# Mixer of a two-layer hybrid diffusion step: S5 gates ahead of the glu products, products out of the state in four bands, result read back on SyncE's queue, convolution branch last

## The chip, the cores and the metric

The kernel runs on one core of one Trainium2 chip. The metric is device time in microseconds (us), the median of several runs of the whole program, lower is better. The engines are PE (TensorE, matrix products), DVE (VectorE), ACT (ScalarE), POOL (GpSimd) and SP (SyncE), which here only issues transfers; ACT and POOL have queues for transfers too.

## What is computed

Two layers over 384 tokens (128 context, 256 latent), width 1024. A layer is half a SwiGLU feed-forward block, a mixer and another half block, each behind a modulated norm. The change lies in the mixer:

```python
def _mixer(h, P, l, h0):
    z = h @ P['w_in'][l]
    z_a, z_b, z_c = jnp.split(z, [S5_WIDTH, S5_WIDTH + 2 * CONV_WIDTH], axis=-1)
    y_a, h_final = _s5_branch(z_a, P, l, h0)      # 512 wide
    y_b = _conv_branch(z_b, P, l)                 # 256 wide, 31 taps, layer norm, silu
    y_c = _sgmlp_branch(z_c, P, l)                # 256 wide
    gates = jax.nn.sigmoid(h @ P['w_gate'][l] + P['b_gate'][l])
    g_a, g_b, g_c = jnp.split(gates, N_BRANCH, axis=-1)
    merged = (g_a * (y_a @ P['w_br_a'][l]) + g_b * (y_b @ P['w_br_b'][l])
              + g_c * (y_c @ P['w_br_c'][l]))
    return merged @ P['w_out'][l], h_final
```

The S5 branch is a complex diagonal state-space scan in both directions over 32 groups of 16 channels with 64 states, then `y = gelu(C s + d*z)` and `y * sigmoid(y @ w_glu)`.

## The kernel before

Every large product is made of three float32r products, high times high, high times low, low times high (L198, L199, L200), over 384 token columns. Weights come in units of 128 x 1024 numbers: SP's queue loads `wr` (512 KB), ACT rounds it to `wh` (L126), DVE subtracts to get `wl` (L105). Each of the three has three buffers, and units are fetched two ahead. A unit is 24 matmuls on PE, or 12 where the contraction is 256 deep (the branches b and c). Within a unit all four k of output block m = 0 come first, then those of m = 1. An activation operand is likewise a pair: `hh`/`hl` (normed input, and later the merged sum), `ah`/`al` (the S5 branch), `yc` and `yb` pairs.

PE's order is the program's. The order on the other engines is a fixed list that the framework's scheduler makes from the program, so a statement that moves in the program can move its rows on DVE and ACT past others.

A mixer's units, numbered from 1: w_in 1 to 12; then for n = 0 to 3 a gate c unit pair and a branch c unit (13 to 24); gate b 25 to 32; then the list `LAST`; then w_out 51 to 58. In `LAST`, "gate" is a pair of units of the S5 gate, "glu" one unit of the S5 output product, "a" and "b" the branch products of S5 and convolution. Before, LAST puts gate 0, 1 in units 33 to 36, glu 0, 1 in 37, 38, gate 2 in 39, 40, a 0, a 1 in 41, 42, gate 3 in 43, 44, a 2 in 45, b 0, b 1 in 46, 47, a 3 in 48, b 2, b 3 in 49, 50. An "a" result is multiplied by its sigmoid gate and added into `acc`, then a "b" result; when a block has both, `hh`/`hl` of it are split off, and w_out needs them in order of k.

Beside the units run the steps of `side()`: after each unit one entry of its `plan` is executed. The S5 scan goes through it in four quarters q of 8 groups: `load_to` (weights `ms`), `to_state` (products L1172 into a bank, then copies into `m_xs`), `rotate` and `scan` on DVE (`m_t`, two scans L1215, L1216, then `m_hh`), `load_from` (weights `my`, `mi`), `from_state` (products L1249, copy `m_ysb` on ACT, transfers to `y_d` in DRAM on ACT's queue and back to `m_yt` on POOL's), `activate` (transposes L138, then y, its gelu, `zp`, `ah`, `al`). The convolution's 31 taps (`cacc`), the longest chain of DVE rows, and its layer norm (`csq`, `csd`, `crs`, `cn`, ending in `yb`) are entries of the plan too. Small products given to `small` are popped one list after each triple of matmuls.

In `from_state` the 48 columns of U or `hh` are stationary and 128 weight columns move, once for each half of the bank:

```python
pe.matmul(b[64 * half : 64 * half + NCH, g * P : (g + 1) * P], u, w, ...)
```

## Time and profile before

| | |
|---|---|
| median of 3 runs | 1775.85 us (1775.21 to 1778.99) |
| profiled execution, its own time | 1775.03 us |
| its span, first to last instruction | 1773.0 us |
| mean granted clock of TensorE | 0.997 |
| PE busy | 1743.7 us, 98% |
| DVE busy | 1246.8 us, 70% |
| ACT busy | 795.8 us, 45% |
| POOL busy | 203.5 us, 11% |
| layer 0's mixer | some 345 to 616 us, with w_out |
| layer 1's mixer | some 1230 to 1490 us |

The profile is of one execution. A busy share is an average over the whole span; a stage can have another limit than the average shows, so the windows and the waits are read beside it. A matmul's listed duration overlaps the next one, so costs on PE are read from start to start.

### The profile page before, as it was taken

The page shows a single profiled execution, that of the slowest core. Times are in us where ns is not written, and L with a number is a line of the kernel's source. Part 1 is how long each engine was busy: PE and PEld are TensorE (multiplying, and loading weights), DVE is VectorE, ACT ScalarE, POOL GpSimd, SP SyncE. Part 2 cuts the span into 40 slices and gives each one's busy share as a digit, 9 for nine tenths or more (in the row PEclk, how much of TensorE's full clock was granted, in tenths as well). Part 3 has the DMA queues.
Part 4 walks back from the last instruction along what each step waited for, and adds up shares of the span by engine and source line. Part 5 has one row for each costly group of instructions (what it writes and reads, how often), then busy time and mean ns, then how long its engine had stood idle before and what let it go on. Part 6 is the DMA issues. An engine that isn't in the chain of part 4 may idle for free.

```text
span 1773.0 us, 30946 instructions
## 1 busy us (share of the span) xinstructions
PE 1743.7 (98%) x12116; PEld 1652.8 (93%) x12116; DVE 1246.8 (70%) x2344; ACT 795.8 (45%) x1330; POOL 203.5 (11%) x400
## 2 busy tenths in 40 slices
PE   7999999999999999999999999999999999999997
PEld 4899999999999989999999899999999999999997
DVE  5496676778986885678487666767799788544435
ACT  3344333575355553233366233336744546423233
POOL 2012343310010000000001133232100000000000
PEclk9999999999999999999999999999999999999999
DMA  9778788776753677788346776667666443444332
GB/s 343 249 224 275 231 252 269 226 198 190 240 157 108 186 238 228 237 280 257 112 131 208 234 224 215 175 195 233 162 210 200 131 123 116 132 130 127 123 125 77
DMA packets 253753, 344.48 MB, mean 194 GB/s; under 512 B 22399, under 2 KB 216651, under 8 KB 253608
## 3 DMA queue, kind: packets, MB, share of 16 engines
q1 hardware_dynamic: 228504, 299.18, 53.4%
q0 software_dynamic: 17088, 39.51, 7.5%
q10 hardware_dynamic: 8016, 3.82, 0.8%
q8 instruction: 95, 1.56, 0.4%
q14 instruction: 50, 0.41, 0.1%
HBM read 309.75 MB, written 32.70 MB: 193 GB/s over the span
## 4 chain that ended last, share of the span: by engine, by line
PE 81%; DVE 10%; ACT 4%; DMA 3%; issue 2%; SPq 0%; ACTq 0%; DVEq 0%
PE mm L198 25%; PE mm L200 25%; PE mm L199 25%; PE ax L386 3%; DVE wl L105 3%; DVE cacc L123 2%; DMA wr<-in_w_gate_dram 1%; DVE m_t L105 1%; PE tb L138 1%; ACT wh L126 1%; DVE m_hh L105 1%; DMA modw<-in_w_mod_dram 1%; DVE macc L123 1%; DMA wr<-in_w_in_dram 1%; ACT zp L1125 0%
## 5 line engine op out<-in xcount | busy, mean ns | idle before, releaser
L105 DVE TENSOR_TENSOR wl<-wr,wh 128x1024 fp32r<-128x1024 f32 (+2 forms) x389 | 457.0, 1175 | 352.1 <-ACT wh L126 347.4
L126 ACT ACTIVATE wh<-wr 128x1024 fp32r<-128x1024 f32 (+1 forms) x387 | 395.9, 1023 | 613.9 <-PE mm L199 443.9
L198 PE MATMUL mm<-hh,wh 128*128 128x384 f32 x1840 | 625.3, 340 | 2.7 <-ACT hh L621 2.7
L200 PE MATMUL mm<-hh,wl 128*128 128x384 f32 x1840 | 617.1, 335 | 4.4 <-DVE wl L105 4.2
L199 PE MATMUL mm<-hl,wh 128*128 128x384 f32 x1840 | 616.3, 335 | 0.5 <-DVE hl L105 0.3
L198 PEld LDWEIGHTS mm<-hh,wh 128*128 128x128 f32 x1840 | 345.9, 188 | 31.7 <-issue 18.1
L200 PEld LDWEIGHTS mm<-hh,wl 128*128 128x128 f32 x1840 | 345.8, 188 | 6.7 <-DVE wl L105 6.7
L199 PEld LDWEIGHTS mm<-hl,wh 128*128 128x128 f32 x1840 | 345.9, 188 | 1.2 <-DVE hl L105 1.1
L198 PE MATMUL mm<-ah,wh 128*128 128x384 f32 x800 | 273.2, 342 | 0.0
L199 PE MATMUL mm<-al,wh 128*128 128x384 f32 x800 | 269.4, 337 | 0.8 <-DVE al L105 0.8
L200 PE MATMUL mm<-ah,wl 128*128 128x384 f32 x800 | 270.0, 338 | 0.0
L198 PEld LDWEIGHTS mm<-ah,wh 128*128 128x128 f32 x800 | 150.2, 188 | 10.2 <-issue 6.7
L199 PEld LDWEIGHTS mm<-al,wh 128*128 128x128 f32 x800 | 150.4, 188 | 1.7 <-DVE al L105 1.1
L200 PEld LDWEIGHTS mm<-ah,wl 128*128 128x128 f32 x800 | 150.2, 188 | 0.0
L123 DVE SCALAR_TENSOR_TENSOR x<-mm,gt,x 128x128 f32<-128x128 f32 x224 | 83.1, 411 | 33.3 <-PE mm L200 33.1
L198 PE MATMUL mm<-xh,wh 128*128 128x386 f32 x240 | 84.7, 353 | 0.0
L126 ACT ACTIVATE ah<-av 128x384 fp32r<-128x384 f32 x82 | 42.1, 519 | 89.4 <-DVE av L105 89.1
L200 PE MATMUL mm<-xh,wl 128*128 128x386 f32 x240 | 81.9, 341 | 0.0
L199 PE MATMUL mm<-xl,wh 128*128 128x386 f32 x240 | 81.9, 341 | 0.0
L123 DVE SCALAR_TENSOR_TENSOR macc<-modw,silu_c,macc 128x1024 f32<-128x1024 f32 x56 | 69.9, 1278 | 14.9 <-DMA modw<-in_w_mod_dram 14.9
L123 DVE SCALAR_TENSOR_TENSOR cacc<-pad,pv,cacc 128x399 f32<-128x399 f32 x120 | 69.7, 627 | 0.0
L386 PE MATMUL ax<-modw,silu_c 128*32 128x512 f32 (+1 forms) x576 | 63.2, 511 | 0.7 <-DMA modw<-in_w_mod_dram 0.7
(316 smaller groups left out, 1820.0 us busy)
## 6 DMA issues: line engine op xcount, KB each, us to landing
wr<-in_ffn_w_dram SPq DMA_DIRECT2D x256, 512.0 KB, 3.6
modw<-in_w_mod_dram SPq DMA_DIRECT2D x144, 512.0 KB, 5.4
wr<-in_w_gate_dram SPq DMA_DIRECT2D x48, 512.0 KB, 3.8
wr<-in_w_in_dram SPq DMA_DIRECT2D x24, 512.0 KB, 3.6
my<-my POOLq DMA_DIRECT2D x16, 512.0 KB, 5.5
ms<-ms POOLq DMA_DIRECT2D x16, 512.0 KB, 4.9
m_ms<-ms SPq DMA_DIRECT2D x16, 512.0 KB
m_my<-my SPq DMA_DIRECT2D x16, 512.0 KB, 7.4
```

The costliest lines, as they stand in the source:

```text
L105: (eng or dve).tensor_tensor(out, a, b, op=op)
L123: dve.scalar_tensor_tensor(out, a, s, b, op0=op0, op1=op1)
L126: act.activation(hi, full, AF.Copy)
L138: pe.transpose(out, in_, ident[:rows, :rows])
L198: pe.matmul(out, wh[:, k, cols], xh, start=first, stop=False)
L199: pe.matmul(out, wh[:, k, cols], xl, start=False, stop=False)
L200: pe.matmul(out, wl[:, k, cols], xh, start=False, stop=last)
L386: pe.matmul(b[32 * s : 32 * s + 32, :w], silu_c[:, k, :], raws[i][:, c : c + w], start=(k == 0), stop=(k == KD - 1), skip_group_check=True,)
```

## The change

- `LAST` runs all four S5 gates first, then glu 0, 1, then a 0 to a 3, then b 0 to b 3. The S5 gates' sigmoids go to a tile of their own pool (`gate_a`).
- `to_state` gives both products to `small` as one list.
- `from_state` makes the weights stationary, 32 columns at a time, in four bands of the bank, and the 48 columns of U or `hh` move: 192 traced matmuls for each q instead of 48. The result already has channels on partitions; one copy and one transfer take it to `y_d`, whose layout is changed.
- `load_y`, a plan entry of its own, reads it back with eight transfers of 24 KB on SP's queue.
- `activate` has no transposes; y reads `m_yt` in SBUF, and the reordering of tokens moves into the write of `zp`.
- The plan is laid out anew: `load_to` ahead of `load_from`, `from_state` for q = 0 to 3 after units 17, 22, 27, 32 (before: 17, 21, 25, 29), `activate` after 22, 27, 32, 37 (before: 25, 27, 30, 33), the convolution's taps spread differently, its mean, variance and broadcast after 38, 41 and 43 (before: 36, 39, 41).

```diff
@@ -1077,8 +1077,8 @@
         return v.rearrange("p (j c) -> p j c", j=TC)
 
     LAST = [
-        ("gate", 0), ("gate", 1), ("glu", 0), ("glu", 1), ("gate", 2), ("a", 0), ("a", 1), ("gate", 3), ("a", 2),
-        ("b", 0), ("b", 1), ("a", 3), ("b", 2), ("b", 3),
+        ("gate", 0), ("gate", 1), ("gate", 2), ("gate", 3), ("glu", 0), ("glu", 1), ("a", 0), ("a", 1), ("a", 2),
+        ("a", 3), ("b", 0), ("b", 1), ("b", 2), ("b", 3),
     ]
 
     def mixer_srcs(l):
@@ -1112,7 +1112,7 @@
 
 
         zd = drm.tile([G, H, TC, NCH], F32, tag=f"z_d{l}", name="z_d")
-        yd = drm.tile([NT, G * H], F32, tag=f"y_d{l}", name="y_d")
+        yd = drm.tile([4, P, GB, NCH], F32, tag=f"y_d{l}", name="y_d")
         ld.start()
         hs = ld.hs
         zp = m6([P, 4, NT], "zp")
@@ -1185,9 +1185,11 @@
                 act.activation(XS[HI, i, :, 1:EC], bv[HI, :, CC - 1 :: -1], AF.Copy)
                 act.activation(XS[HI, i, :, EC + 1 :], bv[HI, :, NCH - 1 : CC - 1 : -1], AF.Copy)
 
+            place = []
             for i in range(2):
                 b = tb_bank()
-                small.append([partial(product, i, g, b) for g in range(GB)] + [partial(take, i, b)])
+                place += [partial(product, i, g, b) for g in range(GB)] + [partial(take, i, b)]
+            small.append(place)
 
         def rotate(q, part):
             d = st5[q]
@@ -1242,44 +1244,38 @@
 
             def product(g):
                 for n in range(3):
-                    for half in range(2):
-                        i = 4 * half + g
-                        u = U[:, q * GB + i, :] if n == 0 else hh[:, n - 1, i, :]
-                        w = mib[:, i, :] if n == 0 else d["my"][i // GS][:, i % GS, n - 1, :]
+                    u = U[:, q * GB + g, :] if n == 0 else hh[:, n - 1, g, :]
+                    w = mib[:, g, :] if n == 0 else d["my"][g // GS][:, g % GS, n - 1, :]
+                    for r in range(0, P, 32):
                         pe.matmul(
-                            b[64 * half : 64 * half + NCH, g * P : (g + 1) * P],
+                            b[r : r + 32, g * NCH : (g + 1) * NCH],
+                            w[:, r : r + 32],
                             u,
-                            w,
                             start=(n == 0),
                             stop=(n == 2),
                             skip_group_check=True,
                         )
 
             def take():
-                ysb = c2([P, TC, 4, H], "m_ysb")
-                bv = b.rearrange("p (g i h) -> p i g h", g=4, h=H)
-                yv = yd.rearrange("(c i) f -> c i f", i=TC)
-                for half in range(2):
-                    r = slice(64 * half, 64 * half + NCH)
-                    act.activation(ysb[r], bv[r], AF.Copy)
-                    f0 = q * P + 64 * half
-                    bq.dma_start(yv[:, :, f0 : f0 + 64], ysb[r].rearrange("c i g h -> c i (g h)"))
-                d["yt"] = c2([P, 3, P], "m_yt")
-                gq.dma_start(d["yt"], yd[:, q * P : (q + 1) * P].rearrange("(t p) f -> p t f", p=P))
-
-            small.append([partial(product, g) for g in range(4)] + [take])
+                ysb = c2([P, GB, NCH], "m_ysb")
+                act.activation(ysb, b[:, : GB * NCH].rearrange("p (g c) -> p g c", c=NCH), AF.Copy)
+                bq.dma_start(yd[q], ysb)
+
+            small.append([partial(product, g) for g in range(GB)] + [take])
+
+        def load_y(q):
+            d = st5[q]
+            d["yt"] = c2([P, TC, NCH], "m_yt")
+            for g in range(GB):
+                tq.dma_start(d["yt"][g * H : (g + 1) * H], yd[q, :, g, :].rearrange("(i h) c -> h i c", h=H))
 
         def activate(t):
-            b = tb_bank()
-            for n in range(3):
-                transpose(b[:, n * P : (n + 1) * P], st5[t]["yt"][:, n, :], P)
             y2 = tmp("y2")
-            ci = lambda v: v.rearrange("p (c i) -> p c i", i=TC)
-            stt(ci(y2), zp[:, t].rearrange("p (j c) -> p c j", j=TC), pv[:, 48 + t : 49 + t], ci(b[:, :NT]))
+            stt(y2, zp[:, t], pv[:, 48 + t : 49 + t], st5[t]["yt"].rearrange("p i c -> p (i c)"))
             ga = tmp("ga")
             gelu_sig(ga, y2)
             yg = zp[:, t]
-            mul(yg, y2, ga)
+            mul(yg.rearrange("p (c i) -> p i c", i=TC), jc(y2), jc(ga))
             ygs[t] = yg
             hl = a_pair()
             split(yg, *hl)
@@ -1477,31 +1473,33 @@
                 [f(sg_u, 0), f(sg_u, 1)],
                 [f(sg_gelu)],
                 [f(to_state, 0), f(sg_norm)],
-                [f(load_from, 0), f(rotate, 0, 0), f(rotate, 0, 1)],
-                [f(load_to, 1), f(scan, 0, 0), f(sg_mix), f(sg_out)],
+                [f(load_to, 1), f(rotate, 0, 0), f(rotate, 0, 1)],
+                [f(load_from, 0), f(scan, 0, 0), f(sg_mix), f(sg_out)],
                 [f(scan, 0, 1)],
-                [f(to_state, 1), tap[0]],
-                [f(load_to, 2), f(rotate, 1, 0), f(rotate, 1, 1)],
-                [f(from_state, 0), f(load_from, 1), f(scan, 1, 0)],
+                [tap[0]],
+                [f(to_state, 1)],
+                [f(load_to, 2), f(from_state, 0), f(rotate, 1, 0), f(rotate, 1, 1)],
+                [f(load_from, 1), f(scan, 1, 0)],
                 [f(scan, 1, 1)],
-                [f(to_state, 2), tap[1]],
-                [f(load_to, 3), f(rotate, 2, 0), f(rotate, 2, 1)],
-                [f(from_state, 1), f(load_from, 2), f(scan, 2, 0)],
+                [f(load_y, 0), tap[1]],
+                [f(to_state, 2), tap[2]],
+                [f(load_to, 3), f(from_state, 1), f(rotate, 2, 0), f(rotate, 2, 1)],
+                [f(load_from, 2), f(scan, 2, 0), f(activate, 0)],
                 [f(scan, 2, 1)],
-                [f(to_state, 3), tap[2]],
-                [f(rotate, 3, 0), f(rotate, 3, 1)],
-                [f(from_state, 2), f(load_from, 3), f(scan, 3, 0)],
-                [f(scan, 3, 1), f(activate, 0)],
-                [tap[3]],
-                [f(activate, 1)],
-                [f(from_state, 3), tap[4]],
-                [f(ctx_states), tap[5]],
-                [f(activate, 2)],
+                [f(load_y, 1), tap[3]],
+                [f(to_state, 3), tap[4]],
+                [f(from_state, 2), f(rotate, 3, 0), f(rotate, 3, 1)],
+                [f(load_from, 3), f(scan, 3, 0), f(activate, 1)],
+                [f(scan, 3, 1)],
+                [f(load_y, 2), tap[5]],
                 [tap[6]],
+                [f(from_state, 3)],
+                [f(ctx_states), f(activate, 2)],
                 [tap[7]],
-                [f(activate, 3), tap[8]],
+                [f(load_y, 3), tap[8]],
                 [tap[9]],
                 [tap[10]],
+                [f(activate, 3)],
                 [f(conv_mean)],
                 [f(conv_center)],
                 [],
@@ -1613,9 +1611,9 @@
         yfs = []
         for op, n in LAST:
             if op == "gate":
-                banks = gate(0, n)
-                for bank, bias in banks:
-                    gt = tmp("gt")
+                gat = c3([P, 2, NT], "gate_a")
+                for m, (bank, bias) in enumerate(gate(0, n)):
+                    gt = gat[:, m]
                     with tc.high_priority():
                         act.activation(gt, bank, AF.Sigmoid, bias=bias)
                     gts.append(gt)
```

The first place is DVE ahead of unit 25, the first unit of gate b 0, in layer 0. `cacc` are taps, `m_t` the rotation, L1217 and L1218 (L1215 and L1216 before) the two scans of one q, `wl` the low halves in order of units; the row of form 128x512 is unit 24. Before:

```order
L105 TENSOR_TENSOR acc<-mm,gt 128x384
L123 SCALAR_TENSOR_TENSOR cacc<-pad,pv_311,cacc 128x399 x4
L105 TENSOR_TENSOR wl<-wr,wh 128x512
L123 SCALAR_TENSOR_TENSOR cacc<-pad,pv_311,cacc 128x399 x3
L105 TENSOR_TENSOR wl<-wr,wh 128x1024
L123 SCALAR_TENSOR_TENSOR cacc<-pad,pv_311,cacc 128x399
L105 TENSOR_TENSOR m_t_5585<-m_rot,m_xs 128x400
```

After, between the same two `wl` (unit 24's is followed by three cacc, by y_5616 of `activate` and by one more cacc; these are the rows from there on):

```order
L105 TENSOR_TENSOR m_t_5455<-m_rot,m_xs 128x400
L105 TENSOR_TENSOR m_t_5456<-m_rot,m_xs 128x400
L105 TENSOR_TENSOR m_t_5457<-m_rot,m_xs 128x400
L105 TENSOR_TENSOR m_t_5455<-m_t_5455,m_t_5456 128x400
L105 TENSOR_TENSOR m_t_5458<-m_rot,m_xs 128x400
L1217 SCALAR_TENSOR_TENSOR m_t_5456<-m_rho,m_t_5455 128x400
L105 TENSOR_TENSOR m_t_5457<-m_t_5457,m_t_5458 128x400
L105 TENSOR_TENSOR m_t_5455<-m_rot,m_t_5456 128x400
L1218 SCALAR_TENSOR_TENSOR m_t_5458<-m_rho,m_t_5457 128x400
L123 SCALAR_TENSOR_TENSOR ga<-ga,y_5616 128x384
L105 TENSOR_TENSOR m_t_5457<-m_rot,m_t_5458 128x400
L105 TENSOR_TENSOR wl<-wr,wh 128x1024
```

Three taps stood between the two `wl` before; now four taps, y, ga and the whole rotation and scan of q = 2 stand there.

The second place is ACT around the glu products in layer 0. `cs` is the sigmoid of a glu product, `ah` the high half of the branch, `csd` the root of the convolution's variance. Before, from glu 0 on:

```order
L1626 ACTIVATE cs<-mm 128x384
L126 ACTIVATE ah<-zp 128x384
L1626 ACTIVATE cs<-mm 128x384
L126 ACTIVATE wh<-wr 128x1024
L126 ACTIVATE ah<-zp 128x384
L1626 ACTIVATE cs<-mm 128x384
L126 ACTIVATE ah<-zp 128x384
L126 ACTIVATE wh<-wr 128x1024
L1443 ACT_TABLE_LOAD
L1443 ACTIVATE csd<-ax,eps_t 128x3
L1620 ACT_TABLE_LOAD
L1620 ACTIVATE gt<-mm,pv_311 128x384
```

After:

```order
L126 ACTIVATE wh<-wr 128x1024
L1618 ACTIVATE gate_a<-mm,pv_311 128x384
L126 ACTIVATE wh<-wr 128x1024
L1439 ACT_TABLE_LOAD
L1439 ACTIVATE csd<-ax,eps_t 128x3
L1624 ACT_TABLE_LOAD
L1624 ACTIVATE cs<-mm 128x384 x2
L126 ACTIVATE wh<-wr 128x1024
L126 ACTIVATE ah<-zp 128x384 x2
L1624 ACTIVATE cs<-mm 128x384 x2
L126 ACTIVATE ah<-zp 128x384 x2
L126 ACTIVATE wh<-wr 128x1024
```

The root of the variance with its two table loads stood behind the four `cs`, with the gates; it now stands ahead of them.

The third place is DVE at the start of w_out, in layer 0. `gate_b` is the product of a "b" result with its gate, `hl` the low halves of the merged sum, in order of k (0, 1, 2, 3, ...). Before, from unit 50's `wl` on:

```order
L105 TENSOR_TENSOR wl<-wr,wh 128x512
L105 TENSOR_TENSOR gt<-mm,gt 128x384
L105 TENSOR_TENSOR hl_6618<-acc,hh_6617 128x384
L105 TENSOR_TENSOR hl_6624<-acc,hh_6623 128x384
L105 TENSOR_TENSOR acc<-acc,gate_b 128x384
L105 TENSOR_TENSOR gt<-mm,gt 128x384
L105 TENSOR_TENSOR acc<-acc,gate_b 128x384
L105 TENSOR_TENSOR gate_b<-mm,gate_b 128x384
L105 TENSOR_TENSOR hl_6650<-acc,hh_6649 128x384
L105 TENSOR_TENSOR hl_6656<-acc,hh_6655 128x384
L105 TENSOR_TENSOR gate_b<-mm,gate_b 128x384
L105 TENSOR_TENSOR wl<-wr,wh 128x1024
```

After, from the product of b 2 on (its first `wl` is unit 51's):

```order
L105 TENSOR_TENSOR gate_b<-mm,gate_b 128x384
L105 TENSOR_TENSOR hl_6942<-acc,hh_6941 128x384
L105 TENSOR_TENSOR hl_6948<-acc,hh_6947 128x384
L105 TENSOR_TENSOR gate_b<-mm,gate_b 128x384
L105 TENSOR_TENSOR wl<-wr,wh 128x1024
L105 TENSOR_TENSOR gate_b<-mm,gate_b 128x384 x2
L105 TENSOR_TENSOR acc<-acc,gate_b 128x384 x2
L105 TENSOR_TENSOR wl<-wr,wh 128x1024
L105 TENSOR_TENSOR hl_6974<-acc,hh_6973 128x384
L105 TENSOR_TENSOR hl_6980<-acc,hh_6979 128x384
```

The pair of `hl` for k = 2, 3 stood ahead of unit 51's `wl`; it now stands behind the last products of b 3, two sums and unit 52's `wl`.

## Rows read from the trace of the kernel before

**Rows 1.** The page: busy time, share of the span and instructions of each engine.

```profile
PE 1743.7 (98%) x12116; PEld 1652.8 (93%) x12116; DVE 1246.8 (70%) x2344; ACT 795.8 (45%) x1330; POOL 203.5 (11%) x400
```

**Rows 2.** Waits of PE: what it waited for, total us, times, longest us.

```profile
PE mm L200 <- DVE wl L105: 4.2, 5, 1.4
```

**Rows 3.** Windows: us, busy us (x instructions) of each engine, granted clock, DMA share, GB/s.

```profile
440.00:520.00 80.00, 77.75 (x774) 73.88 (x773) 79.79 (x145) 35.41 (x65) 9.17 (x15) 1.00 0.63 204
```

**Rows 4.** Timeline, PE, both product bursts: start us, us, engine, line, operation, tiles, form, count.

```profile
399.78 0.33 PE L200 MATMUL mm<-hh,wl 128*128 128x384 f32 x1
...
403.42 0.34 PE L200 MATMUL mm<-hh,wl 128*128 128x384 f32 x1
403.69 0.89 PE L1172 MATMUL tb<-U,m_ms 128*32 128x48 f32 x64
404.50 0.44 PE L198 MATMUL mm<-hh,wh 128*128 128x384 f32 x1
...
432.06 0.34 PE L200 MATMUL mm<-hh,wl 128*128 128x384 f32 x1
...
435.08 0.44 PE L198 MATMUL mm<-hh,wh 128*128 128x384 f32 x1
```

**Rows 5.** Timeline, DVE, one full stretch of layer 0's mixer.

```profile
477.15 0.97 DVE L1216 TENSOR_TENSOR_SCAN m_t<-m_rho,m_t 128x400 f32<-128x400 f32 x1
478.05 1.19 DVE L105 TENSOR_TENSOR wl<-wr,wh 128x1024 fp32r<-128x1024 f32 x1
479.17 0.56 DVE L105 TENSOR_TENSOR m_t<-m_rot,m_t 128x400 f32<-128x400 f32 x1
...
480.12 1.25 DVE L105 TENSOR_TENSOR m_hh<-m_t,m_t 64x128 f32<-64x128 f32 x4
...
485.36 0.91 DVE L123 SCALAR_TENSOR_TENSOR y<-zp,pv,tb 128x384 f32<-128x384 f32 x1
486.18 0.63 DVE L123 SCALAR_TENSOR_TENSOR cacc<-pad,pv,cacc 128x399 f32<-128x399 f32 x1
486.72 1.22 DVE L105 TENSOR_TENSOR wl<-wr,wh 128x1024 fp32r<-128x1024 f32 x1
```

**Rows 6.** Timeline, PE, the wait behind that stretch; [idle before <-releaser].

```profile
485.95 0.34 PE L200 MATMUL mm<-hh,wl 128*128 128x384 f32 x1
486.12 0.49 PE L138 MATMUL tb<-ident,m_yt 128*128 128x128 f32 x3
...
486.62 0.33 PE L199 MATMUL mm<-hl,wh 128*128 128x384 f32 x1
488.00 0.44 PE L200 MATMUL mm<-hh,wl 128*128 128x384 f32 x1 [1.04 <-DVE wl L105]
```

**Rows 7.** Timeline, end of the second glu product: PE, then ACT, then DVE.

```profile
539.17 0.34 PE L200 MATMUL mm<-ah,wl 128*128 128x384 f32 x1
...
539.37 1.06 ACT L126 ACTIVATE wh<-wr 128x1024 fp32r<-128x1024 f32 x1
540.34 0.51 ACT L126 ACTIVATE ah<-zp 128x384 fp32r<-128x384 f32 x1
...
544.62 1.28 ACT L1443 ACT_TABLE_LOAD   x1
...
543.22 0.56 DVE L105 TENSOR_TENSOR al<-zp,ah 128x384 fp32r<-128x384 f32 x1 [0.51 <-ACT ah L126]
```

**Rows 8.** Timeline, DVE, ahead of the output projection.

```profile
579.90 1.01 DVE L105 TENSOR_TENSOR hl<-acc,hh 128x384 fp32r<-128x384 f32 x2
...
581.30 1.22 DVE L105 TENSOR_TENSOR wl<-wr,wh 128x1024 fp32r<-128x1024 f32 x1
```

**Rows 9.** Windows and PE's timeline after the longest wait of layer 0's mixer.

```profile
360.61 0.37 PE L468 MATMUL ax<-ones,sqacc 128*32 128x1 f32 x24 [1.96 <-DVE sqacc L105]
...
360.50:362.00 1.50, 1.40 (x29) 1.38 (x30) 1.50 (x4) 1.21 (x2) 0.00 (x0) 0.81 1.10 397
362.00:364.50 2.50, 2.50 (x9) 2.50 (x8) 2.46 (x8) 0.00 (x0) 0.00 (x0) 0.50 0.74 226
```

## Prediction

> **What bounds the kernel now.** I read the page first: PE is busy 98% of the span [rows 1], so time moves only if PE gets less to do or waits more or less. PE's own waits come next. In the mixers the wait that recurs is for wl, the low half of a weight unit, which DVE makes [rows 2]: 4.2 us over the kernel, nearly all of it in two places, one per layer. The windows say why: from 440 to 520 us DVE is busy 79.79 of 80 us [rows 3]. In that stretch, "the wall" below, PE has next to no lead, and an instruction put in front of a wl is paid by PE. Outside it DVE has room, and what counts there is the length of a chain from one PE result to the next PE operand.
>
> The unit of account: a matmul of 384 columns takes 0.173 us start to start (399.78 to 403.42 us is 21 of them) [rows 4], so a weight unit of 24 takes PE 4.15 us and one of 12 takes 2.08.
>
> **Part 1, less work on PE (gain).** A burst of products pays for a change of shape at both ends: 403.42 to 403.69 is 0.27 instead of 0.173, and about the same again behind it, 0.2 in all; the 64 matmuls between take 0.81 us, 12.7 ns each [rows 4]. Merging the two lists of to_state drops one pair of changes for each of four q: 4 x 0.2 = 0.8. A from_state burst takes 435.08 - 432.06 - 0.17 = 2.85, 2.95 with the change behind it [rows 4]. Its replacement has 192 traced matmuls of exactly the form of the 64 priced above (32 stationary columns, 48 moving): 192 x 12.7 ns + 0.2 = 2.64, so 0.31 less, four times: 1.25. The three transposes of activate cost 486.62 - 485.95 less two matmuls, 0.33 [rows 6], four times: 1.3. Together **-3.4 us per layer**, -6.7 for two. Bounds -2.9 to -3.9: the new form accumulates three products in a bank, which the priced one does not, so I allow 0.5 either way.
>
> The trace shows 12.7 ns for a matmul of this form [rows 4]. The Trainium skill (TensorEngine Tiling (Array Packing), Instruction Overhead) speaks against the change: every matmul carries about 60 cycles of overhead, so one with 48 columns is no faster than one with 60, and a tiling factor should not be taken from a dimension that is already small. By it, cutting 48 products into 192 short ones could cost some 25 ns each (an estimate from that page at 2.4 GHz), which would make the sum +19 us larger. The trace does not agree with it for this form.
>
> **Part 2, the wall (loss).** PE's gain can't be had while DVE is the limit, and the change also moves whose rows stand in front of which wl. Pitches (start to start) from one stretch [rows 5]: wl 1.12, scan 0.90, a 384- or 400-wide operation 0.475, four m_hh 1.25, cacc 0.54, y with its operand in PSUM 0.82. Added up over the 19 rows between the wl at 478.05 and the one at 486.72, these give 7.5 + 1.12 us; the trace has 8.67 [rows 5], and PE waited 1.04 for that wl [rows 6]. So I added up DVE's rows in both orders, unit by unit, against PE's 4.15 or 2.08 plus bursts, with a wl never before its buffer is free (three units back). For the old order this gives 2.7 us of waits a mixer; the trace has 4.2 for two, 2.1 each [rows 2]. For the new order it gives waits of about 2.7 at unit 20, 2.9 at unit 25 and 1.1 at unit 30: 6.8. Unit 25 is the clearest: 16 rows stand between wl(24) and wl(25), 4 cacc, y2 and ga, 8 rotation rows and both scans: 4 x 0.54 + 10 x 0.475 + 2 x 0.90 = 8.7, then wl itself, 9.8 in all, where PE has the 2.08 us unit 24 and a lead of about 5 before that. Before, three cacc stood there. The gains are in this: y2 reads SBUF (0.475 for 0.82), and zp, now written strided, is taken at 0.475 (0.9 if it behaves like y). **+4.1 us per layer**; bounds +1 (the same rows, had they fallen evenly over the units) to +5.5 (zp at 0.9 too).
>
> **Part 3, glu beside a (loss).** Before, gate 2's two units (8.3 us) lay between glu 1 and a 0. The last matmul of glu 1 started at 539.17 and ended the unit at 539.34; the chain sigmoid, product with zp, ah, al was done at 543.22 + 0.56 = 543.78, 4.4 us later [rows 7], and cost nothing under that cover. Now a 0 follows at once, and its fourth k needs al3 at 3 x 0.52 + 0.17 = 1.73 us. Even the old chain would leave a wait of 4.4 - 1.73 = 2.7. The new one is longer: the convolution's variance lands at glu 0's end, so ACT runs wh (1.06), a table load (1.28), csd, a second load, then four cs of some 0.5, and wh(45) and four ah (0.51) with them [rows 7]; its second cs is over just after glu 1's end, and wh(45) at +1.15. DVE then runs wl(45) to 2.3, al0, al1, zp2, zp3 to 4.2, waits for ah3 (4.9) and ends al3 at about 5.45. Wait: 5.45 - 1.73 = **+3.7 us per layer**, bounds 2.7 to 3.8. What is queued behind it on PE is the whole of a; nothing else is there to run.
>
> **Part 4, the start of w_out (loss).** Before, a 3 stood between b 1 and b 2, so the sums for merged rows 2 and 3 were done early: hl2, hl3 at 580.91 and unit 51's wl at 582.5 [rows 8], no wait. Now b 0 to b 3 run in 2.08 us each, DVE's list has both products of b 3, then the sums 2 and 3, then wl(52), then hl2, hl3. From b 3's end: product 0.7, two sums 1.65, wl 2.8, hl2 about 3.5, hl3 about 4.0, against a need at 1.21 and 1.73: **+2.3 us per layer**, bounds 0.6 (wl(51) alone, late by DVE's tally) to 2.4.
>
> **Part 5, at nothing.** y_d in one copy and one DMA instead of two: ACT is busy 35.41 of 80 us in the wall [rows 3], no bound. m_yt as eight short DMAs on SyncE's queue instead of one on GpSimd's: 64 issues among the weight loads; in the order no weight load stands behind a piece that waits for something later than what the load itself needs, and the weights come two units ahead. If the last piece is late, DVE waits with y2 in the wall; one wl's slot, 1.1 us, bounds it. The gates' new pool and place move sigmoids that PE does not wait for. Order of gates 2, 3 costs PE the same 24 matmuls.
>
> **The sum.** -3.4 + 4.1 + 3.7 + 2.3 = +6.7 per layer, +13.4 for two. The profiled run took 1775.03 us, a span of 1773.0 with 2.0 around it; the median of the runs is 1775.85, 0.8 higher. So 1775.0 + 13.4 = 1788.4, and I say **1788**. All lower bounds together: -3.9 + 1 + 2.7 + 0.6 = +0.4 a layer, 1776; all upper: -2.9 + 5.5 + 3.8 + 2.4 = 8.8, 1793.
>
> **Rivals.**
> (a) *Faster: PE's saving comes through.* If the waits in the new order are not where the sum puts them, because DVE's rows shift among themselves and the chains end under the units, what is left is part 1: 1775 - 6.7 = 1768. For it: PE is 98% busy [rows 1] and the saving is work that is surely gone. Against: the wall [rows 3], and the 4.4 us chain, read straight off a trace [rows 7], with 1.73 us of cover.
> (b) *No change: losses as large as the saving.* The wall eats the saving (+3.4) and the chains are half hidden; or all terms lie at their lower bounds: 1774 to 1778.
> (c) *Slower still: the clock.* After PE idled 1.96 us at 358.6 in layer 0's mixer, the granted clock fell to 0.81 and then 0.50, the 1.2 GHz level, until 364.5 us [rows 9]; the half-speed stretch of some 3.6 us gave up about 1.8. The waits of parts 3 and 4 are as long or longer. If each is followed by such a stretch, 4 x 1.8 = 7 more: 1795. It decides from a wait of about 2 us; against it, several waits of about a microsecond in the wall left the clock at 1.00 [rows 3], and parts 3's waits come in pieces with matmuls between.
> (d) *The four-band products dear.* If the bands don't overlap once they accumulate, a product pays by its moving columns as the old ones did: 2.85 us for 48 of 128 columns [rows 4] is 22.3 ns for 48 columns, 9.6 more than 12.7, times 8 x 192: +15, 1803. Against it stands the price of the same form [rows 4]. The Trainium skill's rule under part 1 would add a little more.
>
> **How the numbers follow.** The forecast (1780 to 1793) 0.62; (a) 0.13; (b) 0.11; (c) 0.11; (d) 0.03. Range 1774 to 1796: it takes in all bounds, (b) and most of (c), and leaves (a), (d) and the end of (c) out, under 2 in 10. About 0.2% (3.5 us) is what a measurement of this kernel can tell from no change: faster than 1772.3 is (a), 0.13; within it is (b), 0.11; the rest, 0.76, is slower.
>
> **What would show it.** After the change, PE's waits at the first k of a behind glu 1 should be named al and ah and come to some 3.7 us in each layer, and those at the first unit of w_out hl, some 2.3. The waits for wl should grow from 4.2 to some 13 us, the largest before unit 25. The product burst should read 192 matmuls in 2.4 us, with no transposes of m_yt. If the waits for al and hl are under a microsecond, parts 3 and 4 are wrong; if those for wl don't grow, part 2; if PE's clock row falls below 9 in the mixers, (c) is at work.

## The result, and the profile after

The changed kernel takes 1799.45 us (1798.68 to 1800.22, four runs) against 1775.72 us: ratio 1.0139, 95% interval 1.0124 to 1.0154, 24 us slower. The forecast was 1788, range 1774 to 1796: the right side, half the size.

The page's first lines, of the changed kernel:

```profile
span 1797.3 us, 33227 instructions
...
PE 1750.6 (97%) x13244; PEld 1660.6 (92%) x13244; DVE 1249.2 (70%) x2344; ACT 789.2 (44%) x1322; POOL 196.8 (11%) x392
```

PE is busy 6.9 us more than before [rows 1] and its span is 24.3 us longer; its mean granted clock fell from 0.997 to 0.987. A product that runs at the lower clock counts as busy longer, so part of the loss is hidden in the busy time.

Where it went is read from the starts of the first matmul of named units, in us. Four stretches of a mixer: W, from the first unit of gate c to the first S5 gate (the wall); C, from there to w_out (gates, glu, a, b); D, w_out's first two units; the rest of the changed kernel's two profiles is within 0.6 us of before, but for two waits told under after_again; in the experiments it differs by up to 2.9 us. Column pairs are layer 0 and layer 1. The second profile of the changed kernel (run after_again) is the one to compare; the reason stands with that run.

| kernel | median | W | C | D |
|---|---|---|---|---|
| before | 1775.7 | 97.6, 98.3 | 69.7, 69.7 | 8.4, 8.4 |
| changed, first profile | 1799.5 | 97.3, 100.8 | 74.2, 73.8 | 12.4, 12.4 |
| changed, second profile | 1798.4 | 101.1, 102.6 | 74.0, 73.9 | 12.4, 12.4 |
| a_cover | 1790.5 | 98.3, 103.0 | 69.5, 69.5 | 12.4, 12.5 |
| a_a3 | 1792.3 | 102.2, 102.6 | 75.3, 75.2 | 8.3, 8.4 |
| a_both | 1784.3 | 101.3, 103.6 | 69.5, 69.4 | 8.3, 8.4 |
| a_split4 | 1800.4 | 99.3, 100.5 | 74.9, 76.0 | 12.5, 10.9 |
| b_last | 1792.8 | 98.1, 98.0 | 75.4, 76.4 | 11.0, 10.9 |
| b_bands | 1790.9 | 108.2, 105.6 | 69.4, 69.3 | 8.4, 8.3 |
| b_pool2 | 1779.8 | 101.6, 100.0 | 69.4, 69.6 | 8.4, 8.4 |
| b_pool4 | 1782.6 | 100.2, 103.9 | 69.4, 69.3 | 8.4, 8.4 |
| b_few | 1768.9 | 94.7, 94.4 | 69.7, 69.7 | 8.3, 8.4 |
| both_few | 1772.7 | 95.7, 96.6 | 69.5, 69.4 | 8.4, 8.3 |
| both_split4_few | 1771.2 | 95.2, 94.5 | 69.5, 69.4 | 8.4, 8.4 |

In the second profile W is 3.5 and 4.3 us longer than before, C 4.3 and 4.2, D 4.0 and 4.1: 24.3, less 0.3 us a layer ahead of W, where the first merged list of to_state stands.

PE's waits in the second profile (engine, tile and line, what it waited for: total us, times, longest):

```profile
PE tb L1250 <- issue: 8.3, 5, 2.6
...
PE mm L198 <- ACT gt L1580: 4.5, 2, 3.0
PE mm L199 <- DVE al L105: 3.1, 3, 1.3
...
PE mm L199 <- DVE hl L105: 2.9, 4, 1.1
PE mm L198 <- ACT ah L126: 2.9, 2, 1.4
PE mm L200 <- DVE wl L105: 2.2, 2, 1.4
...
PE mm L198 <- ACT hh L126: 1.9, 2, 1.0
```

Before, the mixers had one recurring row, for wl, 4.2 us [rows 2]. Now the largest has no named releaser ("issue") and lies inside the bursts of products; gt, ah and hh are new, and al and hl (0.8 and 0.3 us before, outside the mixers) now stand in the mixers too.

**The chain behind glu 1.** ACT, DVE, then PE in the changed kernel (first profile); columns are start, duration, engine:

```profile
555.61 1.28 ACT L1439 ACT_TABLE_LOAD   x1
556.90 0.26 ACT L1439 ACTIVATE csd<-ax,eps_t 128x3 f32<-128x3 f32 x1
557.18 1.28 ACT L1624 ACT_TABLE_LOAD   x1
...
559.24 1.06 ACT L126 ACTIVATE wh<-wr 128x1024 fp32r<-128x1024 f32 x1
...
562.99 0.99 ACT L126 ACTIVATE ah<-zp 128x384 fp32r<-128x384 f32 x2 [1.11 <-DVE zp L105]
```

```profile
560.33 1.23 DVE L105 TENSOR_TENSOR wl<-wr,wh 128x1024 fp32r<-128x1024 f32 x1 [0.30 <-ACT wh L126]
561.47 1.02 DVE L105 TENSOR_TENSOR al<-zp,ah 128x384 fp32r<-128x384 f32 x2
562.40 1.02 DVE L105 TENSOR_TENSOR zp<-zp,cs 128x384 f32<-128x384 f32 x2
...
563.55 1.03 DVE L105 TENSOR_TENSOR al<-zp,ah 128x384 fp32r<-128x384 f32 x2
```

```profile
558.98 0.34 PE L200 MATMUL mm<-ah,wl 128*128 128x384 f32 x1
560.76 0.45 PE L198 MATMUL mm<-ah,wh 128*128 128x384 f32 x1 [1.44 <-ACT ah L126]
562.08 0.44 PE L199 MATMUL mm<-al,wh 128*128 128x384 f32 x1 [0.87 <-DVE al L105]
```

The two table loads (1.28 us each) stand on ACT ahead of `cs`, so wh(45) runs at 559.24; the last al ends at 563.55 + 1.03 = 564.58, 5.4 us after glu 1's end at 559.15 (4.4 us before, under cover [rows 7]). PE stops for ah, then for al. What follows shows in the granted clock (the number after the five engines' times):

```profile
560.00:562.50 2.50, 0.87 (x3) 0.61 (x4) 2.20 (x5) 1.88 (x5) 0.00 (x0) 1.00 0.01 3
562.50:566.00 3.50, 3.50 (x12) 2.79 (x11) 2.10 (x6) 0.99 (x2) 0.00 (x0) 0.51 0.24 75
566.00:569.00 3.00, 3.00 (x17) 2.73 (x16) 1.83 (x4) 0.87 (x1) 0.00 (x0) 1.00 0.00 0
```

PE runs at 0.51, the 1.2 GHz level, from 562.5 to 566: only 12 matmuls in 3.5 us, where some 20 fit.

**The start of w_out.** DVE, then PE (first profile):

```profile
589.75 1.01 DVE L105 TENSOR_TENSOR gate_b<-mm,gate_b 128x384 f32<-128x384 f32 x2
590.68 1.01 DVE L105 TENSOR_TENSOR acc<-acc,gate_b 128x384 f32<-128x384 f32 x2
591.62 1.22 DVE L105 TENSOR_TENSOR wl<-wr,wh 128x1024 fp32r<-128x1024 f32 x1
592.75 1.01 DVE L105 TENSOR_TENSOR hl<-acc,hh 128x384 fp32r<-128x384 f32 x2
```

```profile
591.84 0.45 PE L198 MATMUL mm<-hh,wh 128*128 128x384 f32 x1 [0.96 <-ACT hh L126]
593.35 0.69 PE L199 MATMUL mm<-hl,wh 128*128 128x384 f32 x1 [1.07 <-DVE hl L105]
```

DVE takes both products of b 3, two sums and unit 52's wl (591.62) before hl for k = 2, 3 (592.75); PE waits 0.96 us for hh, then 1.07 for hl.

**The wall.** DVE between unit 24's wl and unit 25's, ACT in the same time, and PE's first matmul of unit 25 (first profile):

```profile
461.10 0.69 DVE L105 TENSOR_TENSOR wl<-wr,wh 128x512 fp32r<-128x512 f32 x1
461.70 1.73 DVE L123 SCALAR_TENSOR_TENSOR cacc<-pad,pv,cacc 128x399 f32<-128x399 f32 x3
463.33 0.63 DVE L123 SCALAR_TENSOR_TENSOR y<-zp,pv,m_yt 128x384 f32<-128x384 f32 x1
...
464.41 1.55 DVE L105 TENSOR_TENSOR m_t<-m_rot,m_xs 128x400 f32<-128x400 f32 x3
...
466.84 1.00 DVE L1217 TENSOR_TENSOR_SCAN m_t<-m_rho,m_t 128x400 f32<-128x400 f32 x1
...
468.69 0.99 DVE L1218 TENSOR_TENSOR_SCAN m_t<-m_rho,m_t 128x400 f32<-128x400 f32 x1
469.60 0.54 DVE L123 SCALAR_TENSOR_TENSOR ga<-ga,y 128x384 f32<-128x384 f32 x1
...
470.53 1.23 DVE L105 TENSOR_TENSOR wl<-wr,wh 128x1024 fp32r<-128x1024 f32 x1
```

```profile
470.17 0.52 ACT L1071 ACTIVATE ga<-ga 128x384 f32<-128x384 f32 x1 [3.59 <-DVE ga L123]
470.60 0.56 ACT L1580 ACTIVATE gt<-mm,pv 128x384 f32<-128x384 f32 x1
```

```profile
471.22 0.44 PE L198 MATMUL mm<-hh,wh 128*128 128x384 f32 x1 [2.65 <-ACT gt L1580]
```

461.10 to 470.53 is 9.4 us. PE's wait is booked on ACT's gt, but ACT itself had stood 3.6 us for DVE's ga at 469.60, which is in this queue: the late engine is DVE. In the second profile the same wait is 2.95 us, and the granted clock behind it fell:

```profile
471.00:477.00 6.00, 6.00 (x19) 5.90 (x20) 5.96 (x15) 2.84 (x4) 0.00 (x0) 0.50 0.70 245
```

That is 19 matmuls in 6 us at the 1.2 GHz level, where some 35 fit at 0.173 us.

**The bursts.** One burst of 192 products in the second profile, its end and the windows around it:

```profile
1364.39 0.35 PE L1250 MATMUL tb<-m_hh,m_my 128*32 128x48 f32 x14
1367.34 0.27 PE L1250 MATMUL tb<-m_hh,m_my 128*32 128x48 f32 x2 [2.60 <-issue]
```

```profile
1364.00:1367.30 3.30, 0.74 (x70) 0.60 (x57) 3.30 (x6) 0.00 (x0) 0.00 (x0) 1.00 0.31 68
1367.30:1370.50 3.20, 3.16 (x12) 3.09 (x13) 3.19 (x8) 0.49 (x1) 0.00 (x0) 0.59 0.39 95
1370.50:1373.00 2.50, 2.50 (x14) 2.50 (x13) 2.49 (x8) 0.37 (x1) 0.00 (x0) 0.85 0.87 316
```

After 190 of the 192 products PE stands for 2.6 us and then runs at 0.59. It is no wait for the second tile of weights: that is needed from product 97 on. And the place is fixed: in six profiles of kernels whose PE runs the same instructions up to there in number (the changed kernel twice, a_cover, a_a3, a_both, both_few), the first burst of layer 0 stops after product 113 in five, and in all six the third of layer 0 after 162, the first of layer 1 after 141 or 142 and the third of layer 1 after 190.

### The profile page after: what moved, and what is told of

It reads as the page before. It is cut to its first block, busy times and chain, and to the rows that moved or that the text cites. A ratio compares the mean times of both kernels' runs of the same rounds, so it can differ in the third digit from the quotient of the medians.

```text
span 1797.3 us, 33227 instructions
## 1 busy us (share of the span) xinstructions
PE 1750.6 (97%) x13244; PEld 1660.6 (92%) x13244; DVE 1249.2 (70%) x2344; ACT 789.2 (44%) x1322; POOL 196.8 (11%) x392
## 4 chain that ended last, share of the span: by engine, by line
PE 91%; DMA 3%; DVE 3%; issue 1%; ACT 1%; POOL 0%; SPq 0%; DVEq 0%; ACTq 0%
PE mm L198 28%; PE mm L199 27%; PE mm L200 27%; PE ax L386 3%; PE tb L138 1%; DMA modw<-in_w_mod_dram 1%; PE tb L1250 1%; DVE wl L105 1%; PE tb L1172 1%; DMA U<-z_d 1%; DMA wr<-in_w_in_dram 1%; PE tb L1024 0%; DVE macc L123 0%; ACT wh L126 0%; DMA m_my<-my 0%
## 5 line engine op out<-in xcount | busy, mean ns | idle before, releaser
L123 DVE SCALAR_TENSOR_TENSOR cacc<-pad,pv,cacc 128x399 f32<-128x399 f32 x120 | 69.6, 627 | 0.0
```

Source lines behind the costliest of these rows:

```text
L123: dve.scalar_tensor_tensor(out, a, s, b, op0=op0, op1=op1)
```

## The experiments

Kernels named a_ are the changed kernel with an edit, b_ the kernel before with one; both_ is a_both with one more.

**a_cover**: gate 3 back between glu 1 and a 0.

```diff
-("gate", 2), ("gate", 3), ("glu", 0), ("glu", 1), ("a", 0), ...
+("gate", 2), ("glu", 0), ("glu", 1), ("gate", 3), ("a", 0), ...
```

> The changed kernel, with gate 3's two units put between glu 1 and a 0 again (order gate 0, 1, 2, glu 0, 1, gate 3, a 0 to 3, b 0 to 3); nothing else differs. Theory 1 (the chain from glu's sigmoids to al is exposed, 2.7 us of waits a layer, and a stretch at the half clock behind them costs about 2.4 more): both go, some 5 us a layer, 1789 to 1790 us, no wait for ah or al behind glu 1. Theory 2 (the time between the units is DVE's and ACT's own, waits only move to the next place): less than 3 us gained, 1797 or more, and a new wait of like size in a or b. Theory 3 (the waits are real but the slow clock there has another cause): 5.4 us gained, 1794, and a granted clock still under 1.00 in that stretch.

1790.53 us (1.0084, 1.0052 to 1.0116). C is back at 69.5 us in both layers, 4.5 us gone in each, and no wait for ah or al is left behind glu 1. Theory 1 holds: the waits and the slow clock behind them go together.

**a_a3**: a 3 back between b 1 and b 2.

```diff
-("a", 2), ("a", 3), ("b", 0), ("b", 1), ("b", 2), ("b", 3)
+("a", 2), ("b", 0), ("b", 1), ("a", 3), ("b", 2), ("b", 3)
```

> The changed kernel, with a 3 put between b 1 and b 2 again; nothing else differs. Theory 1 (the sums of merged rows 2 and 3 come too late when b 0 to b 3 stand last: 2.5 us of waits for hh and hl a layer and 1.5 us of half clock behind them): some 4 us a layer gone, 1791 us, no wait for hh or hl at the start of w_out. Theory 2 (DVE has too much to do at that place in any order): less than 2 us gained, and PE still waits for hl or for wl there.

1792.29 us (1.0088, 1.0067 to 1.011). D is 8.33 and 8.35 again, 4.05 us gone in each layer: theory 1.

**a_both**: both edits.

> The changed kernel with both edits to the list: gate 3 between glu 1 and a 0, and a 3 between b 1 and b 2. Theory 1 (the two exposed chains are all that the order of LAST costs): both stages as long as before the change, 69.7 us from the first gate to w_out and 8.35 for w_out's first two units, so 1782 to 1784 us, 7 to 9 above before, and what is left lies in the wall and ahead of it. Theory 2 (the plan itself costs more): over 1786.

1784.3 us (1.0057, 1.0042 to 1.0072), just above theory 1's 1782 to 1784. C and D are as before or a little shorter (no transposes); all that is left, 9 us, lies in W.

**b_last**: the new list alone, in the kernel before.

```diff
-("gate", 0), ("gate", 1), ("glu", 0), ("glu", 1), ("gate", 2), ("a", 0), ("a", 1), ("gate", 3), ("a", 2), ...
+("gate", 0), ("gate", 1), ("gate", 2), ("gate", 3), ("glu", 0), ("glu", 1), ("a", 0), ("a", 1), ("a", 2), ...
-gt = tmp("gt")
+gt = gat[:, m]
```

> The kernel before, with the new order of LAST and the gates' own tiles alone; products, plan of the side work and transfers as before. Theory 1 (the order of LAST by itself exposes both chains, about 5 us behind glu 1 and 4 at w_out in a layer): 18 us slower than before, 1793 to 1795 us. Theory 2 (the chains are exposed only together with the new plan, which puts the convolution's variance at glu 0's end): under 10 us slower, and the wait behind glu 1 is 2.7 us or less a layer, since in this plan the variance comes earlier.

1792.8 us (1.0098, 1.0069 to 1.0127); the traced run is 16.7 us longer than before, 5.7 and 6.7 in C and 2.6 in D of each layer. Theory 1, and theory 2 falls: the wait behind glu 1 is longer here (3.15 us for ah in one piece), though the variance comes earlier; on ACT the convolution's last steps (cn, cs, yb) stand there instead. D shows the clock's part by itself: the same waits of 0.96 and 1.07 us cost 2.6 us here and 4.0 in the changed kernel, where the clock fell behind them (0.71 and 0.76 there). Here it stayed at 1.00.

**a_split4**: each burst in four lists of 48 products.

```diff
-small.append([partial(product, g) for g in range(GB)] + [take])
+small.append([partial(product, g) for g in range(0, 2)])
+small.append([partial(product, g) for g in range(2, 4)])
+small.append([partial(product, g) for g in range(4, 6)])
+small.append([partial(product, g) for g in range(6, 8)] + [take])
```

> The changed kernel, with each from_state burst of 192 products given out as four lists of 48, one behind each triple of the unit, instead of one; nothing else differs. Theory 1 (PE's instructions run out inside a long burst: three of eight bursts stopped after 162 to 190 products for 2.2, 3.2 and 2.6 us, named issue, and half clock followed): those stops go, 8 us of waits and 2 to 3 of clock, against 3 more changes of shape of 0.2 us each for 8 bursts, 4.8: net 5 to 6 gained, 1794 us. Theory 2 (the stops are waits for an operand or a bank that the profile does not name): the stops stay at the same products, and the time rises by up to 4.8, 1800 to 1804 us.

1800.36 us (1.0133, 1.0109 to 1.0156). Neither theory. The stops inside the bursts fell from 8.3 us to 1.7, as theory 1 said, and nothing was gained. Four lists of 48 cost 3.4 us (read under both_split4_few), an undisturbed burst of 192 costs 2.38: 1.0 us more, eight times, 8.2 us, as much as the stops had taken. PE's waits for wl and gt, 5.9 us together, are no longer than the second profile's 6.7. Whether DVE would have taken up a shorter stop in any case is not shown by this run.

**b_few** and **both_few**: taps 3 to 30 left out, in the kernel before and in a_both.

```diff
-tap = [f(conv_taps, j, min(j + 3, CONV_K)) for j in range(0, CONV_K, 3)]
+tap = [f(conv_taps, j, min(j + 3, CONV_K) if j == 0 else j) for j in range(0, CONV_K, 3)]
```

> The kernel before, with the convolution's taps 3 to 30 left out (56 DVE operations of some 0.54 us a layer; the convolution is not computed rightly). Theory 1 (DVE is the wall): DVE falls under 80% between the gates, the waits for wl in the mixers, 2.1 us a layer, go, 1770 to 1772 us. Theory 2 (the waits have another cause): 1775.

> The changed kernel with both edits to the list (as in the run before the last two) and the taps 3 to 30 left out too. Against the kernel before without those taps: Theory 1 (DVE hid PE's saving): with DVE out of the way the saving comes through, 3.4 us a layer, 6 to 7 us faster than that kernel, 1764 us. Theory 2 (bursts of 192 products run out of instructions): some stop for 2 to 3 us and are followed by half clock, so no faster than that kernel, 1770 us or more, with waits named issue inside the bursts.

b_few: 1768.89 us (0.9967, 0.9956 to 0.9978), more gained than theory 1's 1770 to 1772. Its windows:

```profile
420.00:520.00 100.00, 99.76 (x1053) 95.77 (x1052) 73.62 (x132) 49.94 (x90) 9.26 (x16) 1.00 0.64 205
1310.00:1390.00 80.00, 80.00 (x677) 77.84 (x676) 49.45 (x79) 37.39 (x61) 2.94 (x5) 1.00 0.60 195
```

DVE is down to 73.6 of 100 us (99.75 before), PE waits for no engine in W, which is 3 to 4 us shorter. DVE was the limit. So it is in the changed plan: W of both_few is 5.6 and 7.0 us shorter than a_both's.

both_few: 1772.67 us (0.9985, 0.9973 to 0.9997), W 1.0 and 2.3 us longer than b_few's although DVE is out of the way: theory 2. Its bursts stop for 0.8 and 1.9 us in layer 0, 2.0 and 2.3 in layer 1, all "issue", with the granted clock at 0.57 from 483.0 to 486.5 us, behind one of them.

**both_split4_few**: both_few with each burst in four lists.

> The kernel with both edits to the list and without the taps 3 to 30, and each burst of 192 products given out as four lists of 48. Theory 1 (PE runs out of instructions in a long burst; the products themselves are as cheap as the trace shows): no stop of over 0.6 us inside a burst; the stretch from the first gate to the S5 gates goes from 95.7 and 96.6 us to 93.5 (91 plus 4 x 3 x 0.2 for the changes of shape), 1766 to 1768 us. Theory 2 (the four-band products are dear by themselves, or the stops are waits for operands): the stretch stays at 96 or more, 1772 us or more.

1771.16 us (0.9977, 0.9961 to 0.9992). One stop of 0.45 us is left in a burst, and one of 1.0 in an ordinary unit. A list of 48 costs 0.85 us, four cost 3.4, against 2.38 for an undisturbed burst of 192 and 2.96 for the old one. W is that of b_few: splitting ends the stops and costs what the form saves. Theory 1 for the cause; the gain that it promised in W (93.5) did not come.

**after_again**: the changed kernel once more.

> The changed kernel unchanged, for a second profile. If the wait for the state's input (2.8 us, layer 0) and the longer wait for al in the feed-forward part (1.9 us, then half clock) belong to the kernel, both are there again; if they belong to one execution, the time is the same within 2 us and the stops in the wall are longer instead, since the time then given to DVE was what those waits had given it.

1798.37 us. The first profile has a wait of 2.8 us for the state's input U ahead of W in layer 0 (3.9 us with what follows) and a longer one for al in the feed-forward part (2.1 us with what follows). The first is not here and the second is shorter (1.3 us instead of 1.9, at full clock), and the time is the same: W is 3.8 us longer in layer 0 and 1.8 in layer 1 instead. b_shift2, which changes neither transfer, has the wait for U too (0.5 us). So the two, at that length, belong to one execution. The first falls ahead of a stretch that DVE limits; that a late PE gave DVE time there is the reading that fits, from one pair of profiles.

**b_bands**: the kernel before, its plan and LAST, with the merged lists of to_state, the new products, read-back and activate, and the gates' own tiles; `load_y` stands two entries behind `from_state`.

> The kernel before, with its own LAST and plan of the side work, but with the merged products into the state, the four-band products out of it, the result read back on SyncE's queue and no transposes; the read-back stands two entries behind the products. Theory 1 (DVE is the limit in the wall, so PE's saving of 3.4 us a layer turns into waits for DVE there): 1772 to 1776 us, with wl waits up by about what PE saves. Theory 2 (the saving comes through where the plan is not changed): 1768 to 1770 us. Theory 3 (long bursts run out of instructions and cost 2 to 3 us each, with half clock behind): over 1778 us and waits named issue inside the bursts.

1790.94 us (1.0098, 1.0083 to 1.0113): theory 3, and worse. PE's waits:

```profile
PE tb L1172 <- DMA m_ms<-ms: 10.9, 4, 5.7
PE tb L1250 <- issue: 8.4, 4, 3.0
```

Besides the stops, PE waits 10.9 us for m_ms, the weights of to_state, and 4.6 us for m_mi, weights of from_state. Both come through SyncE's queue: in layer 0 it issues eight m_yt from 441.9 to 458.5 us, and the two m_ms behind them go out at 462.59; before, they went at 449.10, in b_pool2 (next) at 451.20.

**b_pool2**, **b_pool4**: b_bands with the read-back on GpSimd's queue and bursts in two and four lists.

```diff
-tq.dma_start(d["yt"][g * H : (g + 1) * H], yd[q, :, g, :].rearrange("(i h) c -> h i c", h=H))
+gq.dma_start(d["yt"][g * H : (g + 1) * H], yd[q, :, g, :].rearrange("(i h) c -> h i c", h=H))
```

> The kernel before, with its own LAST and plan, merged products into the state, four-band products in two lists of 96, no transposes, and the read-back as eight transfers on GpSimd's queue. Theory 1 (the 15 us that the same kernel lost with the read-back on SyncE's queue were its wait for m_ms behind it and stops in long bursts): no wait for m_ms, no long stop, and since y costs DVE 0.3 us less and PE 2.6 us less a layer in a stretch that DVE limits, 1771 to 1775 us. Theory 2 (the old plan doesn't suit the new form, whatever the queue): 1780 us or more, with the wait for m_ms still there.

> As b_pool2, in four lists of 48. If 96 products still outrun PE's instructions, this one is the faster of the two; if not, it is 1 to 2 us slower, by two more changes of shape of 0.2 us in each of eight bursts, as far as DVE does not hide them.

1779.83 us (1.0028, 1.0014 to 1.0041) and 1782.61 (1.0043, 1.0028 to 1.0058). The waits for m_ms are gone, and with the issue times above theory 1 is right on that cause, though this run splits the bursts too; its time is not reached, because the stops remain, in lists of 96 too:

```profile
PE tb L1250 <- issue: 8.5, 5, 2.3
```

96 products do outrun PE's instructions, and b_pool4, which was then to be the faster, is 2.8 us slower: its stops come to 7.1 us against 11.0, but four lists of 48 cost 0.7 us more than two of 96 (3.4 against 2 x 1.36), eight times, and it waits 1.3 us for m_mi. It stops 2.7 us inside a merged to_state burst of 128 and 2.0 us in a list of 48. So the length of a list does not decide where PE stops. Counted over all of PE's matmuls in the trace, it is the place in the stream that does. The number of the matmul behind each stop named "issue" in the mixers:

| kernel | layer 0 | layer 1 |
|---|---|---|
| after_again | 3138, 4031 | 9750, 10133, 10643 |
| both_few | 3138, 3649, 4031 | 9751, 10643 |
| b_pool2 | 3138, 3393, 3776, 4031, 4286 | 9750, 10132, 10387, 10514 |
| b_pool4 | 3138, 3776, 4286 | 10132, 10515 |

The plans and lists differ, the numbers recur. Within a layer the distances (255, 383, 510, 511, 638, 893) are whole multiples of 127.6 matmuls, each with its weight load.

**b_shift**, **b_shift2**: the kernel before, with some taps moved to later entries of the plan (the edit is b_shift's; b_shift2 spreads taps 3 to 10 one or two to an entry).

```diff
-tap = [f(conv_taps, j, min(j + 3, CONV_K)) for j in range(0, CONV_K, 3)]
+at = [0, 3, 5, 7, 9, 11, 13, 15, 18, 21, 25, 28, CONV_K]
+tap = [f(conv_taps, j0, j1) for j0, j1 in zip(at, at[1:])]
 [tap[10]],
+[tap[11]],
 [f(conv_mean)],
```

> The kernel before, with the same 31 taps spread over one more entry of the plan, fewer (two for three) in the entries up to the sixth S5 step of the gates and more behind; the convolution's norm comes one entry later, which its use as an operand has some 8 us to spare for. Theory 1 (DVE's load is the limit in the wall): some 6 us of DVE work a layer leave it, the 2.1 us of waits for wl a layer go in part, 1771 to 1773 us. Theory 2 (it is the order of the rows, not the load): 1774 to 1776 us, the same waits at the same units.

> As b_shift, but with taps 3 to 10 spread one or two to an entry and the norm two entries later. Theory 1: a little more gone, 1770 to 1773 us, if the norm is still ready for b 0; if it is not, a wait for yb at the first convolution unit shows it. Theory 2: 1774 to 1776 us.

1776.1 us (1.0007, 0.9998 to 1.0016) and 1774.49 (0.9998, 0.9989 to 1.0006): no change. The waits for wl stand at the same units, 2.9 and 4.4 us for 4.2. b_shift2's windows:

```profile
420.00:520.00 100.00, 97.75 (x1037) 92.80 (x1036) 99.75 (x184) 46.40 (x86) 9.27 (x16) 1.00 0.61 193
1310.00:1390.00 80.00, 77.26 (x713) 73.69 (x712) 79.00 (x141) 34.83 (x64) 2.94 (x5) 1.00 0.62 198
```

DVE is as full as before (99.75 of 100), so the taps moved in the plan did not lighten the wall: theory 1 is not tried by this, theory 2's times came out. Nothing here beats the kernel before.

## Why the forecast was half of it

**The late chains (parts 3 and 4): waits right, price of the clock left out.** Forecast 3.7 and 2.3 us of waits a layer; PE's starts in the first profile give 3.5 and 2.8 in layer 0. The last al was due 5.45 us after glu 1 and came after 5.43. But C and D cost 4.7 (with the 0.3 us that the transposes save) and 4.1: some 1.2 us more at each place, four places, 5 us (at w_out b_last gives it directly: 4.0 less 2.6, so 1.4). That was rival (c), given 0.11 and entered in the sum at 0; its price of 1.8 a place was too high, its chance much too low. Its argument against itself, that waits in pieces spare the clock, failed: 1.44 and 0.87 us with a few matmuls between were followed by 0.51.

**The wall (parts 1 and 2): the net was +1.0 a layer without the transpose that falls in C, measured +3.1 and +4.0.** Four errors in it.
- Part 1's price was too careful. An undisturbed burst costs 2.38 us, not 2.64, a merged to_state list 1.70 against two of 1.02: 0.58 + 0.34 + 0.33 a q, 5.0 us a layer instead of 3.4. The lists of 48, 64, 96, 128 and 192 products (0.85, 1.02, 1.36, 1.70, 2.38 us) all follow from 0.34 us a list and 10.6 ns a product; the forecast's 12.7 held part of the change of shape, which its 0.2 was too small for. By the Trainium skill's rule (TensorEngine Tiling (Array Packing), Instruction Overhead), about 60 cycles for each matmul, a product would cost some 25 ns (an estimate at 2.4 GHz). The trace does not agree with it.
- What was not foreseen at all is that a burst stops: five times in the second profile, 1.0 to 2.6 us each, 8.3 us in all. I priced 192 products by 64 that ran without a stop. The step that failed is "192 x 12.7 ns": close for the products, wrong for the sequence.
- Part 2's waits came at unit 20 (1.4 us) and unit 25 (3.0, forecast 2.9) in layer 0, 0.8 and 1.5 in layer 1, and none at unit 30: 4.4 and 2.3 instead of 6.8. By the prediction's own sign this part failed: the waits for wl were to grow to some 13 us and came to 2.2 (none in the first profile), and unit 25's are booked on gt. That 3.0 lies so near 2.9 is luck, with 1.5 at the same unit of layer 1. Its starting point was misread too: the 4.2 us for wl before stand at five places, 1.4 us in layer 0 and 2.7 in layer 1, not at one place a layer. Why the waits are shorter than forecast is not shown: the stops give DVE time, but with most of them gone (a_split4) the waits were 3.1 and 2.8. DVE as the limit is shown by b_few and both_few.
- The clock, at 0 in the sum, fell in the wall too: in the second profile to 0.50 from 471 to 477 us and 0.59 from 1350 to 1354.2, behind unit 25's waits, and to 0.51 from 1367.8 to 1371.3, behind the longest stop. That lost some 6.4 us (an estimate: each stretch times the share not granted).

So W and what lies ahead of it add up, for both layers: the new form saved 9.3 us there (10.0 less the transposes in C), the stops cost 8.3, the clock some 6.4, and the waits for wl and gt rose by 2.5 (6.7 for 4.2), while one stop of 0.7 us of before went: about +7.2, measured 7.1. Part 2 had put the waits at +8.2 and the forecast had put the stops and the clock at nothing.

**Part 5.** SyncE's queue cost nothing in the changed plan: PE waits for no m_ms in either of its profiles. In the old plan it does (b_bands, 10.9 us, and 4.6 for m_mi), and not with the read-back on the other queue (b_pool2). "At nothing" held for the plan, not for the edit.

**Rivals.** (a) and (b) are out. (d) is out by the 10.6 ns. (c) came true beside the other terms, at a lower price for each place.

In sum, against the forecast's +13.4 for the traced run: late stretches 16.5 where 11.3 was due (12.0 less the transposes), W and what lies ahead of it 7.1 where 2.1 was due, 0.4 elsewhere: 24.1 with the rounding, the second profile's difference.

**What stops a burst.** The stops lie at the borders of equal pieces of PE's instruction stream (the table under b_pool4). The queue that carries instructions moved, before and after (packets, MB):

```profile
q8 instruction: 95, 1.56, 0.4%
```

and after:

```profile
q8 instruction: 104, 1.70, 0.4%
```

16 KB a packet; 12116 matmuls in 95 packets and 13244 in 104 are 127.5 and 127.3 matmuls, each with its weight load, to a packet: the same piece. In the 2.6 us stop shown above one such packet was moved:

```profile
q8 instruction: 1, 0.02, 2.9%
```

The starts of these packets in the traces settle it. One packet belongs to each border (counted on from a stop). In the eleven traces with the new products, PE passed none of 315 borders around the bursts sooner than 2.2 us after the start of its packet, and in all 52 stops of over 0.15 us at a border it went on 2.2 to 4.2 us after it. So PE stops where it comes to a border before the packet is ready: an ordinary stretch uses up 127.6 matmuls in 22 us, a burst in 1.4. A border inside a burst passes without a stop where its packet started early enough, and lists of 48 help only as far as a border does not fall where much has just been used up.

**What stays open.** What sets the start of a packet: in slow stretches it lies near the border before, in b_pool2 and b_pool4 one started only when PE had come to the border (1346.9 and 1346.8 us). Nor is it shown which waits are followed by the lower clock: 2.65 us ahead of unit 25 was not in the first profile, 2.95 in the second was; 0.96 and 1.07 us at w_out were in one kernel and not in another.

## What to carry to other kernels

A consumer placed right behind the product that feeds it needs the whole chain between them counted, engine by engine and with what else is queued there; unrelated units put between them (gate 3, a 3) were worth 4.5 and 4.05 us a layer here. A price per instruction from a short burst does not hold for one three times as long: short instructions in a row can use up the stream faster than it is loaded. Cutting the row into lists has its own price, 0.34 us a list here. Where another engine is full, what PE saves or loses can be absorbed: take the load off that engine and look again before judging the change.

## What the runs showed of the hardware that was not expected

- PE stops for 0.2 to 3.2 us, with no releaser in the profile, at places of its stream a multiple of 127.6 weight-load and matmul pairs apart, mostly where pairs follow each other every 10.6 ns. It goes on no sooner than 2.2 us after the start of the 16 KB instruction packet that belongs to the place. The kernel before had one such stop, of 0.68 us at 468.
- After some waits of 1 to 3 us the granted clock falls to the 1.2 GHz level for about 3 us, in some cases 7 or more, with 1.2 to 1.5 us lost at each of the late places; after others of the same length it stays at 1.00.
- A wait of PE in one place was made good in the next (U's 3.9 us in layer 0): with DVE full behind it, two profiles that differ by 4 us in a stretch agree in the end (spans of 1797.3 and 1797.0 us).
